# A mixture-of-experts decoder layer on one core: every weight row block split, one activation for the gate, slots found for four experts at a time

## The chip, the cores and the metric

The kernel runs on one core of one Trainium2 chip. The metric is the device time of one execution in microseconds, the median of several runs. The kernel before took 2383.85 us, the median of 3 runs (2383.01 to 2394.71).

## What is computed

One decoder layer over 1024 tokens of width 1024 in float32: a mixer (stick-breaking attention beside causal pooling), cross-attention into 256 memory tokens, and a mixture of experts, each behind an RMSNorm and a residual add; then a last RMSNorm. The change lies in the experts, where each token goes to 4 of 32 experts:

```
gu   = xb @ w1[e] + b1[e]                  # 1024 -> 2048, gate | up
gate = min(gu[:, :1024], 7);  up = clip(gu[:, 1024:], -7, 7)
act  = (up + 1) * gate * sigmoid(1.702 * gate)
y    = (act @ w2[e] + b2[e]) * g           # 1024 -> 1024, g = the routing weight
out[token] += y
```

## The kernel before

The first third of the run is the mixer, the cross-attention and the routing; the change does not touch it but for one scale factor. From about 830 us to the end the kernel goes through the 32 experts in the fixed order `ORDER`, by rank of load (rank 0 has the most tokens; `CAPS` gives each rank its capacity C, from 204 down to 128).

Each expert's weights (12 MB) come as 12 pieces of 1 MB: pieces 0 to 7 of `w1` (each 128 gate and 128 up columns), 8 to 11 of `w2` (256 columns each). A piece has 8 row blocks of 128 rows (index k, `KD` = 8). `load_split` (L1069) issues the load of a piece into a tile `wt` on SP's queue and then makes two parts of the first six row blocks (`KS` = 6): `wh` = the scaled weights in float32r, by ScalarE (L1073), and `wl` = the remainder in float16, by VectorE (L1074). The last two row blocks (`KW` = 2) are used whole, in float32, straight out of `wt`; so `wt` (6 buffers) stays taken until TensorE is through with the piece. `piece` (L1392) issues loads and splits `AHEAD` = 5 pieces ahead of the one that TensorE needs; `wh` and `wl` have 5 buffers each.

The 18 ranks with C over 128 run `ffn_wide` (L1184): weights are stationary, tokens stream. `packed` (L1115) makes one product of 128 output columns: six float32r matmuls over 2C columns (the tokens' high and low part side by side, L1123), six float16 matmuls over C (L1126), two float32 matmuls over C (L1129; each leaves two records in the trace). An expert has 16 such products for gate and up, 8 more for `w2`. Each gate/up product is brought out of PSUM by ScalarE and VectorE (L1198, L1200), clipped (L1203, L1204), gated (`gated`, L1077: a sigmoid on ScalarE, two multiplies on VectorE, L1080 and L1082), and its result parted again for the next product: a float32r copy on ScalarE (L1209), the remainder and a float16 copy on VectorE (L1210, L1055). The two row blocks j = 6, 7 that stay whole end with the gate (L1084). The `w2` products begin with `early` = 3 products over the first `ek` = 5 row blocks, so that the last gates have time to finish.

The other 14 ranks (C = 128) run `ffn_split` (L1256): tokens are stationary, weights stream. `mm_s` (L1132) does three matmuls of 256 columns for each split row block (L1137, L1138, L1139), one float32 matmul for each whole one (L1141, two records).

`prep` (L1352) runs for expert i + 2 at the end of the fourth part of expert i's first product: `slots` (L142) finds which token sits in which slot of the expert (a comparison on VectorE, L144, small matmuls into PSUM, L154, then some nine VectorE instructions of one to three columns for each 128 slots, L160 to L175), and GpSimd gathers the tokens' rows. The rows are transposed and parted for the next expert by `x_T` and `parted` (L1017, L1041; L1049 copies the whole blocks). The instructions' order on each engine is fixed by the tile framework, which simulates the program; `first(n)` raises the priority of what stands in it.

Of the kernel before, what the change touches and what calls it, by code (L numbers as in the profile page):

```python
# [22 lines left out]
P = 128  # L23
# [4 lines left out]
NE = 32  # L28
# [15 lines left out]
           'xg0'), tags=0, BB=(3,), avs=(0, 1), PS=(2, 3, 2), LAG=1, AB=2, GB=(2,), ORD3=range(0, 8), m3=28, mulL=0, x16=1, a16=0, a16L=1, early=3, ek=5, prep=3, wt=6, wh=5, wl=5,  # L44
# [4 lines left out]
KS = 6  # L49
KW = 8 - KS  # L50
# [9 lines left out]
def block_kernel(ctx: ExitStack, tc: tile.TileContext, x, mem, win, gcol, grow, wpool, wout, wqT, wkv, wo,  # L60
# [81 lines left out]
    def slots(C, iota, pcolr, valr, oh, pt, sl, idx, pin=False, later=None, unit=1.0):  # L142

        one = nc.vector.tensor_tensor(oh[:, :, :C], iota[:, None, :C].to_broadcast([P, NB, C]),  # L144
                                      pcolr[:, :, None].to_broadcast([P, NB, C]), op=OP.is_equal)
        if pin:
            tc.keep_in_program_order(one)
# [787 lines left out]
    for i in range(2):  # L935
        r = ORDER[i]
        with tc.issue_after(last.ins):
            S0[i] = slots(CAPS[r], iota_s, posM[:, :, r], lambda b, r=r: vals[:, b, r],
                          sm.tile([P, NB, 256], BF, name="t4", bufs=1) if i else rcs.tile([P, NB, P], BF, name="oh0"),
                          ps.tile([P, 2, 8], F32, name="pl", bufs=2),  # L940
                          rcs.tile([P, 2, 8], F32, name=f"sl{i}"), rcs.tile([P, 2, 2], I32, name=f"idx{i}"), later=later, unit=1.0 / WS)
# [75 lines left out]
    def x_T(sb, q, xg, C):  # L1017

        if general[0]:
            xT = sb.tile([P, KD, P], F32, name="xT")  # L1020
        else:
            xT = sb.tile([P, KS, 2 * C], F32R, name="xT")
            x16 = sb.tile([P, KS, C], F16, name="x16")
            xw = sb.tile([P, KW, C], F32, name="xw")

        def part(g, h):
# [8 lines left out]
            else:  # L1035
                with first(PLAN['hd']):
                    parted(pt[:, :, :m], 4 * h, xT[:, :, o:o + m], xT[:, :, C + o:C + o + m], x16[:, :, o:o + m],
                           xw[:, :, o:o + m], PLAN['x16'])
        return xT if general[0] else (xT, x16, xw), [lambda g=g, h=h: part(g, h) for g in range(len(xg)) for h in range(2)]

    def parted(src, k0, hi, lo, h16, whole, e):  # L1041

        n = max(0, min(4, KS - k0))
        if n:
            ks = slice(k0, k0 + n)
            split(hi[:, ks], lo[:, ks], src[:, :n])
            half(h16[:, ks], hi[:, ks], e)
        if n < 4:
            nc.scalar.activation(whole[:, k0 + n - KS:k0 + 4 - KS], src[:, n:], AF.Copy, scale=WS)  # L1049
# [19 lines left out]
    def load_split(w, src, eng=None):  # L1069
        t = load(w, src, eng)  # L1070
        hi = w.tile([P, KS, 256], F32R, name="wh", bufs=PLAN["wh"])
        lo = w.tile([P, KS, 256], F16, name="wl", bufs=PLAN["wl"])
        last_a[0] = nc.scalar.activation(hi, t[:, :KS], AF.Copy, scale=WS).ins  # L1073
        nc.vector.scalar_tensor_tensor(lo, t[:, :KS], WS, hi.bitcast(F32), op0=OP.mult, op1=OP.subtract)  # L1074
        return hi, lo, t

    def gated(sb, out, g, u, sg, eng=0, unit=None):  # L1077

        nc.scalar.activation(sg, g, AF.Sigmoid, scale=ALPHA)
        nc.vector.scalar_tensor_tensor(u, u, 1.0 - LIM, g, op0=OP.max, op1=OP.mult)  # L1080
        if unit is None:
            (nc.gpsimd if eng else nc.vector).tensor_tensor(out, u, sg, op=OP.mult)  # L1082
        else:
            nc.vector.scalar_tensor_tensor(out, u, unit, sg, op0=OP.mult, op1=OP.mult)  # L1084

    def ffn1(sb, q, w1u, xT, bcol):
        act = sb.tile([P, KD, P], F32, name="act", bufs=1)
        for j in range(8):
# [8 lines left out]
            gated(sb, act[:, j], t[:, 0], t[:, 1], sb.tile([P, 256], F32, name="sg")[:, :P])  # L1097
# [17 lines left out]
    def packed(q, C, part, cs, x, x16, xw, ps=None, ks=range(KD)):  # L1115

# [15 lines left out]
    def mm_s(ps, k, xhi, xlo, x16, xw, part, start, stop):  # L1132

        hi, lo, t = part
        kw = dict(skip_group_check=True)
        if k < KS:
            nc.tensor.matmul(ps, xhi[:, k], hi[:, k], start=start, stop=False, **kw)  # L1137
            nc.tensor.matmul(ps, xlo[:, k], hi[:, k], start=False, stop=False, **kw)  # L1138
            nc.tensor.matmul(ps, x16[:, k], lo[:, k], start=False, stop=stop, **kw)  # L1139
        else:  # L1140
            nc.tensor.matmul(ps, xw[:, k - KS], t[:, k], start=start, stop=stop, **kw)  # L1141
# [42 lines left out]
    def ffn_wide(sb, q, xT, need, r, C, sl, idx, between, last=False):  # L1184

        xT, x16, xw = xT
        act = sb.tile([P, KS, 2 * C], F32R, name="act", bufs=1)
        a16 = sb.tile([P, KS, C], F16, name="a16", bufs=1)
        aw = sb.tile([P, KW, C], F32, name="aw", bufs=1)
        for c in range(4):  # L1190
            for f in range(2):
# [3 lines left out]
                for g in range(2):  # L1195
                    ph = packed(q, C, part, slice(g * P, g * P + P), xT, x16, xw)
# [5 lines left out]
                with first(PLAN['hb']):  # L1202
# [40 lines left out]
        for eh in range(2):  # L1243
# [12 lines left out]
    def ffn_split(sb, q, xT, need, r, C, sl, idx, between, last=False):  # L1256
# [10 lines left out]
        def act_T(c):  # L1267
# [4 lines left out]
            if c % 2:  # L1272
                with first(PLAN['hf']):
                    parted(acts[-1][:, :, :C], 2 * c - 2, aT[:, 0], aT[:, 1], a16, aw,
                           PLAN['a16E'] if last else PLAN['a16L'])
        for c in range(4):
            ph = q.tile([P, 512], F32, name="qh", bufs=5)[:C]
            nc.tensor.matmul(ph, sel, b1hl[:, c], start=True, stop=False, skip_group_check=True)
            for h in range(2):
                part = need(2 * c + h)  # L1280
                for k in range(KD):
                    mm_s(ph[:, h * 256:h * 256 + 256], k, xT[:, :, :C], xT[:, :, C:], x16, xw, part, False,
                         h == 1 and k == KD - 1)
                settle()
            with first(PLAN['he']):
# [6 lines left out]
                gated(sb, ac, t[:, 0], t[:, 1], sb.tile([P, 256], F32, name="sg")[:C], PLAN["mulL"])  # L1292
# [11 lines left out]
        def products(eh, h, kh):  # L1304
# [4 lines left out]
            for k in range(4 * kh, 4 * kh + 4):  # L1309
                mm_s(py[eh][:, h * 256:h * 256 + 256], k, aT[:, 0], aT[:, 1], a16, aw, parts[eh, h], h == k == 0,  # L1310
# [227 lines left out]
```

## Time and profile before

| what | value |
|---|---|
| median of 3 runs | 2383.85 us |
| profiled execution | 2387.4 us, of which the span 2385.8 us |
| experts' stretch | about 830 us to the end |
| granted TensorE clock, mean | 0.972 |

PE is TensorE's matmuls, PEld its weight loads, DVE VectorE, ACT ScalarE, POOL GpSimd, SP the engine that issues most loads. Busy times of one engine in a stretch count overlapping instructions once; a row of grouped instructions gives the sum and the mean time of one, where neighbours can overlap.

### The profile page before, as it was taken

Reading aid. Unit: us, or ns where it says so; the run is one execution under the profiler, and the core shown is the slowest. Engines: PE = TensorE matmul, PEld = TensorE weight load, DVE = VectorE, ACT = ScalarE, POOL = GpSimd, SP = SyncE. Lnnn points to the kernel's source line nnn. Section 1 sums busy time; section 2 is a strip of 40 time slices with the busy share of each in tenths; the row PEclk is TensorE's granted clock in tenths of the full one; section 3 lists DMA queues with packets and bytes.
Section 4 is the critical chain, followed back from the end, with each engine's and each line's share of the span. In section 5 each row is a group of like instructions: output and inputs, shape, how many; then the busy total and the mean of one; then the engine's idle time right before and its main releaser. Section 6 shows DMA issues by size and latency. Waiting matters only on the chain. (4 is left out here: it accounts for less than half of the span.)

```text
span 2385.8 us, 44846 instructions
## 1 busy us (share of the span) xinstructions
PE 2233.9 (94%) x17218; PEld 2031.2 (85%) x17218; DVE 1685.1 (71%) x3716; ACT 1333.7 (56%) x2318; POOL 456.7 (19%) x387
## 2 busy tenths in 40 slices
PE   8999998899899889999999999999999999999985
PEld 7989886689899779988988889987988988888874
DVE  6752878764755667867887677776777777766775
ACT  6633565443542356656666566664666656655653
POOL 2101566543340000111010101101101101011001
PEclk9999999899999889999999999999999999999998
DMA  7821113154322368978778977987888788878785
GB/s 254 278 82 54 45 45 88 58 168 162 113 89 98 146 233 328 316 281 324 299 269 296 323 302 289 329 306 255 298 288 310 276 291 309 285 263 308 264 316 180
DMA packets 100461, 549.90 MB, mean 230 GB/s; under 512 B 14309, under 2 KB 18533, under 8 KB 48401
## 3 DMA queue, kind: packets, MB, share of 16 engines
q1 hardware_dynamic: 74016, 478.71, 53.6%
q0 software_dynamic: 15872, 46.21, 8.1%
q10 hardware_dynamic: 10354, 22.06, 2.6%
q8 instruction: 137, 2.24, 0.4%
q14 instruction: 82, 0.67, 0.1%
HBM read 493.16 MB, written 49.57 MB: 227 GB/s over the span
## 5 line engine op out<-in xcount | busy, mean ns | idle before, releaser
L1074 DVE SCALAR_TENSOR_TENSOR wl<-wt,wh 128x1536 f16<-128x1536 f32 x384 | 673.0, 1754 | 319.6 <-ACT wh L1073 308.8
L1073 ACT ACTIVATE wh<-wt 128x1536 fp32r<-128x1536 f32 x384 | 568.7, 1482 | 320.7 <-DMA wt<-w 291.9
L1123 PE MATMUL qh<-xT,wh 128*128 128x332 f32 (+17 forms) x1728 | 320.0, 321 | 5.6 <-ACT wh L1073 2.4
L1123 PEld LDWEIGHTS qh<-xT,wh 128*128 128x128 f32 x1728 | 255.0, 191 | 8.0 <-DVE gu L1200 3.3
L1137 PE MATMUL qh<-wh,xT 128*128 128x256 f32 x672 | 255.9, 382 | 0.6 <-ACT wh L1073 0.5
L1012 POOL DMA_INDIRECT xg<-Hdr,idx x50 | 58.4, 1168 | 805.2 <-DVE sl L175 322.2
L1129 PE MATMUL qh<-xw,wt 128*128 128x166 f32 (+17 forms) x1152 | 210.2, 304 | 0.0
L1126 PEld LDWEIGHTS <-wl 128*128 128x128 f16 x2592 | 173.1, 99 | 42.1 <-issue 4.6
L1101 POOL DMA_INDIRECT Adr<-y,idx x50 | 104.6, 2091 | 497.0 <-ACT y L1236 186.4
L1139 PE MATMUL qh<-wl,x 128*128 128x256 f16 x672 | 192.3, 286 | 6.7 <-DVE wl L1074 6.5
L1123 PE MATMUL qh<-act,wh 128*128 128x332 f32 (+17 forms) x864 | 179.0, 335 | 20.2 <-DVE act L1210 20.1
L1138 PE MATMUL qh<-wh,xT 128*128 128x256 f32 x672 | 191.5, 285 | 1.2 <-DVE xT L103 1.2
L1126 PE MATMUL qh<-x,wl 128*128 128x166 f16 (+17 forms) x1728 | 168.7, 231 | 0.0
L96 PE MATMUL pd<-uhi,Thi 128*128 128x256 f32 x576 | 165.7, 288 | 1.5 <-DVE x L617 1.1
L97 PE MATMUL pd<-ulo,Thi 128*128 128x256 f32 x576 | 163.7, 284 | 0.0
L1129 PEld LDWEIGHTS qh<-xw,wt 128*128 128x128 f32 x1152 | 162.5, 191 | 0.1
L98 PE MATMUL pd<-uhi,Tlo 128*128 128x256 f32 x576 | 162.5, 282 | 0.0
L1123 PEld LDWEIGHTS qh<-act,wh 128*128 128x128 f32 x864 | 134.6, 197 | 23.9 <-DVE act L1210 22.8
L1137 PEld LDWEIGHTS qh<-wh,xT 128*128 128x128 f32 x672 | 135.8, 202 | 13.9 <-issue 7.3
L1138 PEld LDWEIGHTS qh<-wh,xT 128*128 128x128 f32 x672 | 131.1, 195 | 3.9 <-DVE xT L103 1.5
L1137 PE MATMUL qh<-wh,act 128*128 128x256 f32 x336 | 124.0, 378 | 1.4 <-ACT act L102 1.4
L1198 ACT ACTIVATE gu<-qh,b1P 128x166 f32<-128x166 f32 (+17 forms) x288 | 104.7, 379 | 24.3 <-PE qh L1129 23.2
(398 smaller groups left out, 5506.2 us busy)
## 6 DMA issues: line engine op xcount, KB each, us to landing
wt<-w SPq DMA_DIRECT2D x382, 1024.0 KB
w<-wkv SPq DMA_DIRECT2D x8, 1024.0 KB
uw<-wout SPq DMA_DIRECT2D x16, 512.0 KB
uw<-Mdr SPq DMA_DIRECT2D x16, 512.0 KB
w<-win SPq DMA_DIRECT2D x5, 1024.0 KB
xt<-x SPq DMA_DIRECT2D x8, 512.0 KB
w<-wqT SPq DMA_DIRECT2D x4, 1024.0 KB
Mdr<-st ACTq DMA_DIRECT2D x8, 512.0 KB
```

The lines of the kernel that those rows point to most:

```text
L96: nc.tensor.matmul(ps, whi, mhi, start=start, stop=False, **kw)
L97: nc.tensor.matmul(ps, whi, mlo, start=False, stop=False, **kw)
L98: nc.tensor.matmul(ps, wlo, mhi, start=False, stop=stop, **kw)
L1073: last_a[0] = nc.scalar.activation(hi, t[:, :KS], AF.Copy, scale=WS).ins
L1074: nc.vector.scalar_tensor_tensor(lo, t[:, :KS], WS, hi.bitcast(F32), op0=OP.mult, op1=OP.subtract)
L1123: nc.tensor.matmul(ps[:, :2 * C], part[0][:, k, cs], x[:, k], start=k == 0, stop=False, **kw)
L1126: nc.tensor.matmul(ps[:, :C], part[1][:, k, cs], x16[:, k], start=False, stop=False, **kw)
L1129: nc.tensor.matmul(ps[:, :C], part[2][:, k, cs], xw[:, k - KS], start=False, stop=k == KD - 1, **kw)
L1137: nc.tensor.matmul(ps, xhi[:, k], hi[:, k], start=start, stop=False, **kw)
L1138: nc.tensor.matmul(ps, xlo[:, k], hi[:, k], start=False, stop=False, **kw)
L1139: nc.tensor.matmul(ps, x16[:, k], lo[:, k], start=False, stop=stop, **kw)
L1198: nc.scalar.activation(t[:, g], ph[:, C:2 * C], AF.Identity, scale=1.0 / WS, bias=b1P[:, 8 * g + j, r:r + 1])
```

## The change

All eight row blocks of a piece are split (`KS`, `KW`, the whole tiles `xw`, `aw` and the float32 matmuls go). Loads and splits are separated: splits run 5 pieces ahead as before, loads 8 ahead, and `wt` has 4 buffers in place of 6, given back after the split. The gate is one Silu on ScalarE and one VectorE instruction; its factor 1/1.702 is put into the routing weight (`GU`). The float16 copy of the wide experts' activations moves from VectorE to ScalarE (`a16=1`). Slots are found for four experts in one PSUM tile: one expert's comparison and small matmuls in each of four experts' third part (`mark`), and one set of nine VectorE instructions for all four (`settle_set`).

```diff
-           'xg0'), ... mulL=0, x16=1, a16=0, a16L=1, early=3, ek=5, prep=3, wt=6, wh=5, wl=5,
+           'xg0'), ... mulL=0, x16=1, a16=1, a16L=1, early=3, ek=5, prep=3, wt=4, wh=5, wl=5, ahead=8,
-KS = 6
-KW = 8 - KS
+GU = 1.0 / (WS * ALPHA)
+SLOT_SETS = [[2, 3]] + [list(range(i, i + 4)) for i in range(4, 32, 4)]
...
-    def load_split(w, src, eng=None):
-        t = load(w, src, eng)
-        hi = w.tile([P, KS, 256], F32R, name="wh", bufs=PLAN["wh"])
-        lo = w.tile([P, KS, 256], F16, name="wl", bufs=PLAN["wl"])
-        last_a[0] = nc.scalar.activation(hi, t[:, :KS], AF.Copy, scale=WS).ins
-        nc.vector.scalar_tensor_tensor(lo, t[:, :KS], WS, hi.bitcast(F32), op0=OP.mult, op1=OP.subtract)
-        return hi, lo, t
-    def gated(sb, out, g, u, sg, eng=0, unit=None):
-        nc.scalar.activation(sg, g, AF.Sigmoid, scale=ALPHA)
-        nc.vector.scalar_tensor_tensor(u, u, 1.0 - LIM, g, op0=OP.max, op1=OP.mult)
...
+    def split_w(w, t):
+        hi = w.tile([P, KD, 256], F32R, name="wh", bufs=PLAN["wh"])
+        lo = w.tile([P, KD, 256], F16, name="wl", bufs=PLAN["wl"])
+        last_a[0] = nc.scalar.activation(hi, t, AF.Copy, scale=WS).ins
+        nc.vector.scalar_tensor_tensor(lo, t, WS, hi.bitcast(F32), op0=OP.mult, op1=OP.subtract)
+        return hi, lo
+    def gated(out, g, u, sg):
+        nc.scalar.activation(sg, g, AF.Silu, scale=ALPHA)
+        nc.vector.scalar_tensor_tensor(out, u, 1.0 - LIM, sg, op0=OP.max, op1=OP.mult)
...
         for k in ks:
-            if k < KS:
-                nc.tensor.matmul(ps[:, :2 * C], part[0][:, k, cs], x[:, k], start=k == 0, stop=False, **kw)
+            nc.tensor.matmul(ps[:, :2 * C], part[0][:, k, cs], x[:, k], start=k == 0, stop=False, **kw)
         for k in ks:
-            if k < KS:
-                nc.tensor.matmul(ps[:, :C], part[1][:, k, cs], x16[:, k], start=False, stop=False, **kw)
-        for k in ks:
-            if k >= KS:
-                nc.tensor.matmul(ps[:, :C], part[2][:, k, cs], xw[:, k - KS], start=False, stop=k == KD - 1, **kw)
+            nc.tensor.matmul(ps[:, :C], part[1][:, k, cs], x16[:, k], start=False, stop=k == KD - 1, **kw)
...
-                    if j < KS:
-                        ac = sb.tile([P, 256], F32, name="ac", bufs=PLAN["ac"])[:, :C]
-                        gated(sb, ac, t[:, 0], t[:, 1], sg)
-                        nc.scalar.activation(act[:, j, :C], ac, AF.Copy)
-                        nc.vector.tensor_tensor(act[:, j, C:], ac, act[:, j, :C].bitcast(F32), op=OP.subtract)
-                        conv(PLAN['a16'], a16[:, j], ac)
-                    else:
-                        gated(sb, aw[:, j - KS], t[:, 0], t[:, 1], sg, unit=WS)
+                    ac = sb.tile([P, 256], F32, name="ac", bufs=PLAN["ac"])[:, :C]
+                    gated(ac, t[:, 0], t[:, 1], sg)
+                    nc.scalar.activation(act[:, j, :C], ac, AF.Copy)
+                    nc.vector.tensor_tensor(act[:, j, C:], ac, act[:, j, :C].bitcast(F32), op=OP.subtract)
+                    conv(PLAN['a16'], a16[:, j], ac)
...
+        def mark(n, m):
+            if m == 0:
+                found[n] = q.tile([P, 4, 2, 8], F32, name="qs")
+                nc.tensor.matmul(found[n].rearrange("p m g c -> p (m g c)"), none[:, :P], none[:, :64], start=True,
+                                 stop=False, skip_group_check=True)
...
+            tc.keep_in_program_order(nc.vector.tensor_tensor(
+                oh, iota_s[:, None, :C].to_broadcast([P, NB, C]), posM[:, :, r, None].to_broadcast([P, NB, C]),
+                op=OP.is_equal))
+            for g in range((C + P - 1) // P):
+                w = min(P, C - g * P)
+                for b in range(NB):
+                    nc.tensor.matmul(found[n][:w, m, g, :6], oh[:, b, g * P:g * P + w], vals[:, b, r], start=False,
+                                     stop=False, skip_group_check=True)
+        def settle_set(n):
+            pt = found.pop(n)
+            sl = sb.tile([P, 4, 2, 8], F32, name="sl", bufs=3)
+            idx = sb.tile([P, 4, 2, 2], I32, name="idx", bufs=3)
+            nc.vector.tensor_copy(sl[:, :, :, :3], pt[:, :, :, :3])
+            nc.vector.tensor_scalar(sl[:, :, :, 3:6], pt[:, :, :, 3:6], GU, None, op0=OP.mult)
...
         def piece(i, j):
-            emit(i * 12 + j + 1 + AHEAD)
+            upto = i * 12 + j + 1 + AHEAD
+            while todo_s and todo_s[0][0] * 12 + todo_s[0][1] < upto:
+                n = todo_s.pop(0)
+                emit(n[0] * 12 + n[1] + 1)
+                pieces[n] = split_w(w, loaded.pop(n))
+            emit(i * 12 + j + 1 + PLAN["ahead"])
             return pieces.pop((i, j))
```

## Rows read from the trace of the kernel before

**Rows 1.** The page: span, busy time of each engine, SP's DMA queue (packets, MB, share).
```profile
span 2385.8 us, 44846 instructions
PE 2233.9 (94%) x17218; PEld 2031.2 (85%) x17218; DVE 1685.1 (71%) x3716; ACT 1333.7 (56%) x2318; POOL 456.7 (19%) x387
q1 hardware_dynamic: 74016, 478.71, 53.6%
```
**Rows 2.** Busy time by stretch: length, PE, PEld, DVE, ACT, POOL, clock, DMA share, GB/s.
```profile
830.00:880.00 50.00, 39.07 (x252) 31.89 (x251) 30.52 (x47) 28.09 (x35) 5.14 (x6) 0.79 0.72 267
...
2330.00:2386.00 56.00, 29.89 (x199) 25.19 (x197) 31.10 (x84) 20.47 (x39) 11.52 (x8) 0.80 0.52 171
sum 1556.00, PE 1463.42 PEld 1324.44 DVE 1156.28 ACT 944.92 POOL 173.41; mean PE 292.68 PEld 264.89 DVE 231.26 ACT 188.98 POOL 34.68
...
1260.70:1308.60 47.90, 45.80 (x419) 43.36 (x418) 38.13 (x92) 31.42 (x59) 4.53 (x3) 1.00 0.80 283
1308.60:1387.80 79.20, 76.52 (x578) 65.74 (x576) 58.02 (x98) 46.72 (x61) 9.00 (x5) 1.00 0.86 317
```
**Rows 3.** Waits of PE from 880 to 2340 us: total, times, longest.
```profile
PE qh L1123 <- DVE act L1210: 20.1, 10, 4.5
```
**Rows 4.** Timeline of PE in one wide expert, C = 148: start us, us, instructions.
```profile
1291.87 0.92 PE L1123 MATMUL qh<-act,wh 128*128 128x296 f32 x5
...
1292.92 0.92 PE L1123 MATMUL qh<-act,wh 128*128 128x296 f32 x5
...
1296.28 0.40 PE L1123 MATMUL qh<-act,wh 128*128 128x296 f32 x1 [2.10 <-DVE act L1210]
...
1304.98 1.07 PE L1123 MATMUL qh<-act,wh 128*128 128x296 f32 x6
1305.90 0.57 PE L1126 MATMUL qh<-a,wl 128*128 128x148 f16 x6
1306.30 0.71 PE L1129 MATMUL qh<-aw,wt 128*128 128x148 f32 x4
1306.75 1.07 PE L1123 MATMUL qh<-act,wh 128*128 128x296 f32 x6
```
**Rows 5.** Timeline of PE in one split expert.
```profile
1505.71 1.03 PE L1141 MATMUL qh<-wt,xw 128*128 128x256 f32 x4
...
1506.85 0.36 PE L1137 MATMUL qh<-wh,xT 128*128 128x256 f32 x1
...
1507.21 0.36 PE L1137 MATMUL qh<-wh,xT 128*128 128x256 f32 x1
...
1508.73 1.03 PE L1141 MATMUL qh<-wt,xw 128*128 128x256 f32 x4
```
**Rows 6.** Groups of DVE and ACT, 830 us on: busy, mean ns | idle before, releaser.
```profile
L1074 DVE SCALAR_TENSOR_TENSOR wl<-wt,wh 128x1536 f16<-128x1536 f32 x384 | 673.0, 1754 | 319.6 <-ACT wh L1073 308.8 <-PE qh L1139 4.7 <-ACT gu L1198 2.8
L1073 ACT ACTIVATE wh<-wt 128x1536 fp32r<-128x1536 f32 x384 | 568.7, 1482 | 320.7 <-DMA wt<-w 291.9 <-PE qh L1138 8.2 <-PE qh L1123 6.5
...
L1080 DVE SCALAR_TENSOR_TENSOR gu<-gu 128x256 f32<-128x256 f32 (+18 forms) x200 | 68.5, 342 | 2.0
...
L1209 ACT ACTIVATE act<-ac 128x166 fp32r<-128x166 f32 (+17 forms) x108 | 35.0, 325 | 16.3 <-DVE ac L1082 14.9 <-PE qh L1138 0.9
...
L1055 DVE CAST a<-ac 128x166 f16<-128x166 f32 (+17 forms) x108 | 25.8, 240 | 0.3
...
L160 DVE COPY sl<-qs 128x3 f32<-128x3 f32 (+17 forms) x47 | 5.5, 147 | 1.6 <-PE qs L154 1.5
...
L1079 ACT ACT_TABLE_LOAD x1 | 1.3, 1283 | 0.0
```
**Rows 7.** Timeline of DVE in the wide expert of rows 4.
```profile
1286.60 0.30 DVE L1080 SCALAR_TENSOR_TENSOR gu<-gu 128x148 f32<-128x148 f32 x1
1286.83 0.23 DVE L1055 CAST a<-ac 128x148 f16<-128x148 f32 x1
1286.97 0.30 DVE L1210 TENSOR_TENSOR act<-ac,act 128x148 fp32r<-128x148 f32 x1
...
1288.00 1.75 DVE L1074 SCALAR_TENSOR_TENSOR wl<-wt,wh 128x1536 f16<-128x1536 f32 x1
1289.67 0.23 DVE L1204 TENSOR_SCALAR gu<-gu 128x148 f32<-128x148 f32 x1
```

More of the change, by code (lines that the diff above doesn't have):

```diff
@@ L43 @@
            a16E=1, fb=((0, 1, 2), (3, 4), (5, 6), (7,)), fn=('xg1', 'y1', 'xg0', 'y0', 'xg1', 'y1', 'xg1',
-           'xg0'), tags=0, BB=(3,), avs=(0, 1), PS=(2, 3, 2), LAG=1, AB=2, GB=(2,), ORD3=range(0, 8), m3=28, mulL=0, x16=1, a16=0, a16L=1, early=3, ek=5, prep=3, wt=6, wh=5, wl=5,
+           'xg0'), tags=0, BB=(3,), avs=(0, 1), PS=(2, 3, 2), LAG=1, AB=2, GB=(2,), ORD3=range(0, 8), m3=28, mulL=0, x16=1, a16=1, a16L=1, early=3, ek=5, prep=3, wt=4, wh=5, wl=5, ahead=8,
            gu=2, ac=4)
@@ L140, in bcast_row, with slots @@
         return t
[L142 to L147, printed above, removed]
+    def slots(C, iota, pcolr, valr, oh, pt, sl, idx, later=None, unit=1.0):
+        nc.vector.tensor_tensor(oh[:, :, :C], iota[:, None, :C].to_broadcast([P, NB, C]),
+                                pcolr[:, :, None].to_broadcast([P, NB, C]), op=OP.is_equal)
         ng = (C + P - 1) // P
@@ L1037, in part, with parted @@
                     parted(pt[:, :, :m], 4 * h, xT[:, :, o:o + m], xT[:, :, C + o:C + o + m], x16[:, :, o:o + m],
[L1038 to L1049, printed above, removed]
+                           PLAN['x16'])
+        return xT if general[0] else (xT, x16), [lambda g=g, h=h: part(g, h) for g in range(len(xg)) for h in range(2)]
+    def parted(src, k0, hi, lo, h16, e):
+        ks = slice(k0, k0 + 4)
+        split(hi[:, ks], lo[:, ks], src)
+        half(h16[:, ks], hi[:, ks], e)
     def conv(e, out, src):
@@ L1113, in ffn2, with packed @@
         scatter(ys, idx, 0, P)
-    def packed(q, C, part, cs, x, x16, xw, ps=None, ks=range(KD)):
+    def packed(q, C, part, cs, x, x16, ps=None, ks=range(KD)):
         if ps is None:
@@ L1246, in ffn_wide @@
             cs = lambda e: slice(e % 2 * P, e % 2 * P + P)
-            early = {e: packed(q, C, parts[e // 2], cs(e), act, a16, aw, None, range(PLAN['ek'])) for e in range(PLAN['early'] if eh == 0 else 0)}
+            early = {e: packed(q, C, parts[e // 2], cs(e), act, a16, None, range(PLAN['ek'])) for e in range(PLAN['early'] if eh == 0 else 0)}
             for e in range(4):
-                py = packed(q, C, parts[e // 2], cs(e), act, a16, aw, early.get(e), range(PLAN['ek'] if e in early else 0, KD))
+                py = packed(q, C, parts[e // 2], cs(e), act, a16, early.get(e), range(PLAN['ek'] if e in early else 0, KD))
                 with first(PLAN['hc']):
@@ L1352, in prep @@
         def prep(i):
-            r = ORDER[i]
             if i in S0:
                 S[i] = S0[i]
-            else:
-                S[i] = slots(CAPS[r], iota_s, posM[:, :, r], lambda b: vals[:, b, r], *slot_tiles(sb, q), pin=True,
-                             unit=1.0 / WS)
-            XG[i] = gather(sb, S[i][1], CAPS[r])
+            XG[i] = gather(sb, S[i][1], CAPS[ORDER[i]])
+        found, when = {}, {}
+        for n, s_ in enumerate(SLOT_SETS):
+            for m in range(len(s_)):
+                at = [(0, m), (1, m)][n] if n < 2 else (s_[0] - 6 + m, 2)
+                when.setdefault(at, []).append(lambda n=n, m=m: mark(n, m))
+            when.setdefault([(0, 2), (2, 1)][n] if n < 2 else (s_[0] - 3, 2), []).append(lambda n=n: settle_set(n))
@@ L1367, in block_kernel @@
         pieces = {}
-        todo = [(i, j) for i in range(NE) for j in range(12)]
+        loaded = {}
+        todo, todo_s = ([(i, j) for i in range(NE) for j in range(12)] for _ in range(2))
         def expert_id(i):
@@ L1409, in between @@
                     XT[i + 1], todo_x[:] = x_T(sb, q, XG[i + 1], CAPS[ORDER[i + 1]])
+                for f in when.get((i, c), []):
+                    f()
                 if c == PLAN['prep']:
@@ L1461, in block_kernel @@
                 nc.vector.tensor_sub(g_x, g_x, vx[:, :, 3 + c])
[L1462 removed]
+            sl, idx = slots(P, iota_s, pos_x, lambda b: vx[:, b], *slot_tiles(sb, q), unit=1.0 / ALPHA)
             xT, parts = x_T(sb, q, gather(sb, idx, P), P)
```

68 lines of the change are left out of this document (36 added, 32 removed).

## The prediction, written before the changed kernel was run

> **What bounds the kernel now.** I began with the page's busy line and its span, then took busy times by stretch. From 830 us to the end TensorE (PE) is busy 1463 of 1556 us, VectorE (DVE) 1156, ScalarE (ACT) 945 [rows 1, 2]. Of PE's 93 idle us, 11 lie in the first 50 us and 26 in the last 56; the 1450 us between hold 56. So the experts go at PE's pace, and DVE and ACT have room on the mean. The list of PE's waits says where the 56 us are: 20 us, the largest item, in 10 stops where the second product of a wide expert waits for the last parted activations, the longest 4.5 us [rows 3]. I call that place the handover. The groups by line show ACT idle 292 us before a split for the weights' landing and DVE idle 309 us behind ACT [rows 6]; neither reaches PE as a wait of that size, because splits run five pieces ahead. DMA is 80% busy in a wide expert and 86% in a pair of split ones [rows 2]. The fine timeline of PE then gives the price of each kind of matmul.
>
> **PE, wide experts.** A product with six split and two whole blocks takes 1306.75 - 1304.98 = 1.77 us, of which the four float32 records take 0.45 from their start to the next product [rows 4]. What eight split blocks cost stands in the trace too, since the early products run five split blocks and nothing else: 1292.92 - 1291.87 = 1.05 us, 0.21 a block [rows 4]. Three more blocks: the six float32r matmuls take 0.92 and the six float16 ones 0.40, 0.22 a block together, so 1.05 + 0.66 = 1.71 at most. The first float32r matmul of a run carries a start-up that further ones don't: 5 of them last 0.92 from the first start to the last end, 6 last 1.07, so one more is at most 0.15, and the streamed columns alone (296 and 148 at 2.4 GHz, the granted 1.00) are 0.185; with 0.20 the product is 1.65. Saved: 0.06 to 0.15 us; I take 0.11. There are 18 experts x 24 = 432 products, and the mean C (152.6) is near this 148: 432 x 0.11 = 48 us (26 to 65).
>
> **PE, split experts.** From float32 group to float32 group a piece takes 1508.73 - 1505.71 = 3.02 us, and one split block 1507.21 - 1506.85 = 0.36 [rows 5]. Eight blocks make 2.88; saved 0.14 us on 14 x 12 = 168 pieces, 23 us (18 to 28, as the handover from float32 back costs more or less). PE in all: -71 us, of 1463. Transposes and slot matmuls stay in number, but for one empty matmul a set (eight in all).
>
> **DVE.** A split grows from 1536 to 2048 elements. The row gives 1754 ns; in proportion that adds 585 ns; against the 0.30 us of a 148-element instruction of the same operation [rows 7] the slope is 1.05 ns an element, adding 536. I take 0.54: 384 x 0.54 = +207 us. The gate loses one of two instructions, 68 us; the float16 copies leave, 26 us [rows 6]. Two row blocks more per wide expert need a remainder: 36 x 0.30 = +11. Of x_T and of the split experts' activations the second half has four blocks for two: 64 x 256 elements x 1.05 ns = +17. Nine small slot instructions for each of 47 groups at 0.147 us, 62 us, become nine for each of eight sets, 14 at 0.2 us (they are wider): -48. Net +93: 1249.
>
> **ACT.** The split: 1482 ns, in proportion +494; against 325 ns at about 153 elements [rows 6] +428. I take 0.43: +165 us. Float16 copies for 144 row blocks and 36 new float32r copies at 0.325: +58. Silu for Sigmoid: same shape, 0. Two copies in place of one whole copy at x_T: +5. Net +228: 1173. If DVE and ACT were hidden behind PE as before, all this is free; the cover is PE's time. In a wide expert one row block j costs PE 2 x 1.66 = 3.32 us. DVE's, start to start [rows 7]: split 1.67 + 0.54, two PSUM reads, one gate instruction and one remainder at 0.23, two clips at 0.14 (the float16 copy's spacing): 3.41. Before it was 1.67 + 4 x 0.23 + 2 x 0.14 + 0.75 x (0.14 + 0.23) = 3.15 against PE's 3.54. So in the first product DVE goes from faster than PE to about even, and regains it in the second, where a piece needs no gate. That is thin cover.
>
> **What is late next: the handover.** PE's early products cover it as before: three of 1.05 us. Row blocks 6 and 7 now leave the gate by one DVE instruction less (-0.30) but then need a float32r copy on ACT (+0.33) and a remainder on DVE (+0.30): +0.33 us bare. Each new hop can stand behind a split, now about 1.9 us on ACT and 2.3 on DVE; with the engines 78% and 83% busy, half a split at that chance is 0.74 + 0.95. So +0.3 to +2.0 us in each of 18 wide experts, 6 to 36; I take 20. The same in split experts is wider by 256 elements on both engines: 14 x 0.3 = 4. For other queueing on fuller engines I take 4 more (0 to 30).
>
> **Loads.** Before, a load waited for PE to finish the piece six back. Now it waits for the split of the piece four back, and the split for PE's piece five back; loads reach eight pieces ahead. Queued on SP behind such a load are later loads, the reload of expert numbers and, near the end, result rows; on ACT, behind a split that waits for `wh`, the PSUM copies (L1198) that free PE's five buffers. I take 0: landing waits shift to waits for PE's buffers, and PE has four split pieces in hand. Bounds: -25 (more room between the wide and the split experts' demand removes half of the 56 us) to +30. The slots come earlier and gathers with them; no PE wait in the rows is theirs: 0. Other tiles' sizes: 0.
>
> **Sum.** 2387.4 - 48 - 23 + 20 + 4 + 4 = 2344 for an execution like the profiled one, which lies 3.5 us above the median of the runs; on the median's scale 2341. PE would then be 1392 of about 1513 us, DVE 83%, ACT 78%.
>
> **A rule against it.** The trace has a single table load in this part, 1.283 us, ahead of the first Sigmoid, and after it copies, scaled copies and Sigmoid mix without another [rows 6]. The Trainium skill ("ScalarE: Activation LUTs", "Table sets: the hidden batching unit") says functions come in sets, a change of set costs a load, and cheap ones such as copy and identity are in every set; it doesn't list Silu's. By its last part the change is free, which is the sum above; if Silu's set lacked the copies, it is the last rival.
>
> **Rivals.**
> 1. The new depth pays: handovers don't get longer (DVE rid of 48 us of slot work, PE never short of split pieces) and half the 56 us go. 2384 - 71 - 5 = 2308 to 2315. For it: the 292 us that ACT spends on landings. Against: DVE even with PE. Chance 0.18.
> 2. DMA takes over in the split experts. A 1 MB piece costs 0.536 x 2385.8 / 478.71 x 1.0486 = 2.80 us at full use [rows 1]; a split expert's share of 0.86 over 39.6 us is 34 us of transfers, with gathers and scatters. At 37.9 us that is 0.90. If no more than the present 0.86 can be had there, the split experts' 23 us are lost, and some 8 for unevenness: 2341 + 23 + 8 = 2372. Against: deeper loads even it out. Chance 0.11.
> 3. The handover eats the gain: each of 18 wide experts stops for the longest seen, 4.5 us, 81 us for 20: 2384 - 71 + 61 = 2374, no change. Chance 0.10.
> 4. Slower: DVE becomes the bound of the wide experts' first product. Its place is the eight row blocks at 3.41 us and the comparison and transposed halves (about 3 us) against PE's 26.6 and transposes; from the point where DVE's block exceeds PE's, PE runs out of its five buffers and then waits at the handover for all of DVE's backlog. At 4.5 + 2.0 us per wide expert it is 117 - 20 = 97 us, and half of the 384 splits 0.1 us late 19: 2384 - 71 + 97 + 19 = 2429 at worst, 2400 in the middle. It decides where DVE's spacing is over some 3.5 us a block. Chance 0.09.
> 5. Table changes: two loads of 1.283 us for each of 200 gates put 513 us on ACT, 1686 for 1556: about 2384 + 170 = 2550. Chance 0.02.
>
> **How the numbers follow.** The forecast (2325 to 2360) has 0.50. A measurement tells 0.5%, about 12 us, from no change, so faster means below 2372: the forecast, rival 1 and half of rival 2, 0.74 in all; same is rival 3 and the rest of 2, 0.15; slower is 4 and 5, 0.11. The range for 8 in 10 is 2305 (all of PE's saving and the recovered waits) to 2385.
>
> **What would show it.** PE's wide products 1.66 us apart and a split piece at 2.88; L1074 and L1073's successors at about 2.29 and 1.91 us, 384 each; no second table load; PE's waits for the last remainders 35 to 45 us in total; ACT's idle for landings far under 292. I am wrong if a product saves under 0.06 us, if DVE is over 90% busy in wide experts with PE waits over 100 us, or if DMA is over 0.9 busy with PE waiting for `wh` and `wl`.

## The result: no gain, 0.6% slower

The changed kernel takes 2403.33 us (median of 7 runs, 2396.41 to 2408.48), the kernel before 2387.39 beside it: a ratio of 1.0064 (95% interval 1.0045 to 1.0083). The forecast was 2341. The page after, as in [rows 1], and the stretch from 830 us, as the sum in [rows 2]:

```profile
span 2400.3 us, 45219 instructions
PE 2191.6 (91%) x17562; PEld 1988.5 (83%) x17562; DVE 1806.0 (75%) x3094; ACT 1527.2 (64%) x2434; POOL 502.4 (21%) x387
q1 hardware_dynamic: 74016, 478.71, 54.1%
```
```profile
880.00:1380.00 500.00, 458.19 (x4029) 413.90 (x4029) 411.52 (x626) 365.65 (x547) 66.64 (x67) 0.96 0.80 290
...
sum 1572.00, PE 1418.02 PEld 1279.58 DVE 1278.51 ACT 1139.70 POOL 218.58; mean PE 283.60 PEld 255.92 DVE 255.70 ACT 227.94 POOL 43.72
```

PE works 45 us less, DVE 122 more, ACT 195 more, and the span is 14.5 us longer. PE's unit prices are the predicted ones. Timelines of PE (start, duration): a wide product at C = 148 follows the one before after 1291.44 - 1289.77 = 1.67 us (forecast 1.66; before 1.77), and a split block comes 0.37 us after the one before (0.36 in the median), eight to a piece. Over all 18 wide experts, first products at full clock and without a stop follow each other 0.10 us sooner than before on the mean; such pieces of the split experts take 2.91 us for 3.04 in the median.

```profile
1289.77 1.33 PE L1111 MATMUL qh<-xT,wh 128*128 128x296 f32 x8
1290.94 0.70 PE L1113 MATMUL qh<-x,wl 128*128 128x148 f16 x8
1291.44 1.33 PE L1111 MATMUL qh<-xT,wh 128*128 128x296 f32 x8
```
```profile
1334.98 0.36 PE L1120 MATMUL qh<-wh,xT 128*128 128x256 f32 x1
...
1335.35 0.36 PE L1120 MATMUL qh<-wh,xT 128*128 128x256 f32 x1
```

The groups of DVE and ACT, as in [rows 6] (busy, mean ns | idle before, releaser):

```profile
L1068 DVE SCALAR_TENSOR_TENSOR wl<-wt,wh 128x2048 f16<-128x2048 f32 x384 | 875.2, 2285 | 169.7 <-ACT wh L1067 165.6 <-PE qh L1113 3.1
L1067 ACT ACTIVATE wh<-wt 128x2048 fp32r<-128x2048 f32 x384 | 732.7, 1913 | 172.8 <-PE qh L1121 68.4 <-DMA wt<-w 56.4 <-PE qh L1111 39.2
L1074 DVE SCALAR_TENSOR_TENSOR ac<-gu,sg 128x256 f32<-128x256 f32 (+18 forms) x200 | 67.1, 339 | 1.8 <-ACT sg L1073 0.5
L1073 ACT ACT_TABLE_LOAD x1 | 1.3, 1283 | 0.0
```

The splits cost what was expected, and ACT's idle for landings went from 292 to 56 us. There is still one table load in this part. The Trainium skill ("ScalarE: Activation LUTs", "Table sets: the hidden batching unit") says that cheap functions such as copy and identity are in every set; the single load agrees with that, and shows it beside Silu, which the section's list of sets doesn't name.

What changed is who makes PE wait (880 to 2340 us: total, times, longest):

```profile
PE qh L1111 <- DVE gu L1180: 32.7, 20, 3.1
PE qh L1111 <- DVE act L1189: 15.9, 18, 4.1
PE qs L1343 <- DVE oh L1337: 10.1, 10, 4.6
PE qt L1212 <- DVE yT L1229: 9.9, 14, 1.0
```

The longest single stop comes late, behind this window, and ends at 2355 us: PE waits there for ACT to write a wide expert's `y`. The kernel before has none like it:

```profile
PE qt L1247 <- ACT y L1213: 10.9, 1, 10.9
```

The handover, feared in the forecast (35 to 45 us), fell from 20.1 us [rows 3] to 15.9. The new first item is PE's five buffers, freed by DVE's read L1180; before, that item (L1200) was 2.2 us. One such stop, in DVE's and then PE's timeline:

```profile
1250.61 2.28 DVE L1068 SCALAR_TENSOR_TENSOR wl<-wt,wh 128x2048 f16<-128x2048 f32 x1
1252.81 0.28 DVE L1074 SCALAR_TENSOR_TENSOR ac<-gu,sg 128x130 f32<-128x130 f32 x1
1253.02 2.28 DVE L1068 SCALAR_TENSOR_TENSOR wl<-wt,wh 128x2048 f16<-128x2048 f32 x1
1255.22 0.28 DVE L1189 TENSOR_TENSOR act<-ac,act 128x130 fp32r<-128x130 f32 x1
1255.42 0.48 DVE L1180 SCALAR_TENSOR_TENSOR gu<-qh,gu 128x130 f32<-128x130 f32 x2
```
```profile
1255.85 1.95 PE L1111 MATMUL qh<-xT,wh 128*128 128x260 f32 x8 [2.24 <-DVE gu L1180]
...
1260.38 1.20 PE L1111 MATMUL qh<-xT,wh 128*128 128x260 f32 x8
```

Two splits stand back to back, the reads wait behind them, and PE stops for 2.24 us. Then the same eight matmuls take 1.95 us for 1.20. The windows of 1 us show why (length, PE, PEld, DVE, ACT, POOL, clock, DMA, GB/s): PE is busy 0.15 us in the first, and the granted clock stands at 0.50 (1.2 GHz) for the next three.

```profile
1255.00:1256.00 1.00, 0.15 (x1) 0.18 (x2) 1.00 (x6) 0.19 (x2) 0.00 (x0) 0.99 0.99 414
1256.00:1257.00 1.00, 1.00 (x6) 1.00 (x7) 1.00 (x7) 0.00 (x0) 0.90 (x1) 0.50 1.08 451
...
1260.00:1261.00 1.00, 1.00 (x14) 1.00 (x14) 1.00 (x1) 0.87 (x4) 0.00 (x0) 1.00 0.66 213
```

The whole of this wide expert's first product before and after (windows from its first to its last float32r matmul, columns as above):

```profile
1215.40:1242.30 26.90, 26.90 (x272) 25.91 (x271) 22.93 (x60) 20.92 (x43) 4.60 (x2) 1.00 1.00 342
```
```profile
1231.20:1261.60 30.40, 28.16 (x277) 26.80 (x276) 27.28 (x49) 26.38 (x51) 5.79 (x3) 0.94 0.95 347
```

DVE's work in it rose from 22.9 to 27.3 us, more than the 26.9 that the stretch lasted before, when PE never stopped in it.

**The balance.** From 830 us to PE's last matmul, PE's idle time grew from 71.2 to 123.8 us (+53). The time at 1.2 GHz grew from 62.3 to 118.8 us, and what PE was busy of it from 54.4 to 98.3 us. If half of that is lost, as at half the clock, matmuls took 22 us longer (an estimate). Less that, PE's work fell by 45 + 22 = 67 us (forecast 71; from the unit prices above, 432 x 0.10 + 168 x 0.13 = 65). From PE's last matmul to the end it is 28.5 us for 21.1, +7. In sum -67 + 53 + 22 + 7 = +15, the change of the span.

### The profile page after: what moved, and what is told of

Same layout as the page of the kernel before. It is cut to its first block, busy times and chain, and to the rows that moved or that the text cites. A ratio compares the mean times of both kernels' runs of the same rounds, so it can differ in the third digit from the quotient of the medians.

```text
span 2400.3 us, 45219 instructions
## 1 busy us (share of the span) xinstructions
PE 2191.6 (91%) x17562; PEld 1988.5 (83%) x17562; DVE 1806.0 (75%) x3094; ACT 1527.2 (64%) x2434; POOL 502.4 (21%) x387
## 3 DMA queue, kind: packets, MB, share of 16 engines
q8 instruction: 140, 2.29, 0.4%
## 5 line engine op out<-in xcount | busy, mean ns | idle before, releaser
L1068 DVE SCALAR_TENSOR_TENSOR wl<-wt,wh 128x2048 f16<-128x2048 f32 x384 | 875.2, 2285 | 169.7 <-ACT wh L1067 165.6
L1067 ACT ACTIVATE wh<-wt 128x2048 fp32r<-128x2048 f32 x384 | 732.7, 1913 | 172.8 <-PE qh L1121 68.4
L1111 PE MATMUL qh<-xT,wh 128*128 128x332 f32 (+17 forms) x2304 | 407.0, 318 | 32.0 <-DVE gu L1180 31.8
L1111 PEld LDWEIGHTS qh<-xT,wh 128*128 128x128 f32 x2304 | 336.4, 193 | 37.3 <-issue 32.2
L1120 PE MATMUL qh<-wh,xT 128*128 128x256 f32 x896 | 334.9, 375 | 6.7 <-ACT wh L1067 6.7
L1122 PE MATMUL qh<-wl,x 128*128 128x256 f16 x896 | 258.0, 288 | 6.2 <-DVE wl L1068 6.2
L1121 PE MATMUL qh<-wh,xT 128*128 128x256 f32 x896 | 256.7, 287 | 3.4 <-DVE xT L104 3.4
L1111 PE MATMUL qh<-act,wh 128*128 128x332 f32 (+17 forms) x1152 | 229.3, 333 | 16.9 <-DVE act L1189 15.9
L1111 PEld LDWEIGHTS qh<-act,wh 128*128 128x128 f32 x1152 | 180.4, 201 | 23.0 <-DVE act L1189 20.1
L1120 PEld LDWEIGHTS qh<-wh,xT 128*128 128x128 f32 x896 | 183.5, 205 | 16.2 <-ACT wh L1067 7.8
L1121 PEld LDWEIGHTS qh<-wh,xT 128*128 128x128 f32 x896 | 176.7, 197 | 4.6 <-DVE xT L104 3.6
L1120 PE MATMUL qh<-wh,act 128*128 128x256 f32 x448 | 159.6, 368 | 0.8 <-ACT act L103 0.8
L1122 PE MATMUL qh<-wl,a 128*128 128x256 f16 x448 | 128.0, 288 | 1.9 <-DVE wl L1068 1.9
L1121 PE MATMUL qh<-wh,act 128*128 128x256 f32 x448 | 128.9, 294 | 0.8 <-DVE act L104 0.8
L1122 PEld LDWEIGHTS <-x 128*128 128x128 f16 x896 | 87.2, 97 | 39.0
```

The lines of the kernel that those rows point to most:

```text
L1067: last_a[0] = nc.scalar.activation(hi, t, AF.Copy, scale=WS).ins
L1068: nc.vector.scalar_tensor_tensor(lo, t, WS, hi.bitcast(F32), op0=OP.mult, op1=OP.subtract)
```

## The experiments

Ratios are to the kernel before on the same chip, in brackets the 95% interval. The theory at first: DVE's and ACT's fuller queues hold up PE. The rivals: the loads, the slots or the gate.

**The parts alone, with six split blocks.**

```diff
-        nc.scalar.activation(sg, g, AF.Sigmoid, scale=ALPHA)
-        nc.vector.scalar_tensor_tensor(u, u, 1.0 - LIM, g, op0=OP.max, op1=OP.mult)
...
+        nc.scalar.activation(sg, g, AF.Silu, scale=ALPHA)
+        nc.vector.scalar_tensor_tensor(out, u, (unit or 1.0) * (1.0 - LIM), sg, op0=OP.max, op1=OP.mult)
```


> The kernel before with the Silu gate alone (six of eight row blocks split, slots as before). Theory A, long splits queue in front of the PSUM reads: VectorE has 68 us less to do and no split grows, so PE's waits shrink a little, 2372 to 2387 us. Rival B, the gate or the slot sets cost the time by their order on the engines: 2395 or more here or in the next run. PE's waits for the PSUM reads (none over 3 us in total in the kernel before) stay under 5 us by A.

Measured 2371.05 us, 0.9921 [0.9897, 0.9944], just under theory A's range.

```diff
-                S[i] = slots(CAPS[r], iota_s, posM[:, :, r], lambda b: vals[:, b, r], *slot_tiles(sb, q), pin=True,
-                             unit=1.0 / WS)
...
+        def mark(n, m):
+        def settle_set(n):
...
+                for f in when.get((i, c), []):
+                    f()
```


> The kernel before with the slot sets alone. Theory A: some 40 us less on VectorE, no split grows, 2374 to 2388 us. Rival B: the comparisons and small matmuls of a set stand at places where PE waits for them (10 us of waits of L1343 for L1337 in the changed kernel, each followed by a stretch at the half clock), 2395 or more.

Measured 2377.55 us, 0.9949 [0.9933, 0.9965], as by theory A.

Both edits together:

> The kernel before with the Silu gate and the slot sets, six of eight row blocks split. Theory A: over 100 us less on VectorE and all splits as short as before: 2362 to 2383 us, the fastest so far. Rival B: 2395 or more. Rival C, PE's own time with the whole float32 blocks is the bound and no relief of VectorE helps: 2380 to 2390.

Measured 2355.98 us, 0.9856 [0.9823, 0.9889], under all ranges. Each part pays, and they add up. What is left of the change, eight split blocks with the loads in two steps and the float16 copy on ACT, turns 0.9856 into 1.0064: it costs about 50 us. With six blocks neither the gate nor the slots cost time. With eight, PE's waits for the slots' comparisons come to 10.1 us, for 0.2 us here; no run takes the sets alone out of the changed kernel.

**The splits in halves, with eight blocks.** Both lines, or one of the two:

```diff
-        last_a[0] = nc.scalar.activation(hi, t, AF.Copy, scale=WS).ins
-        nc.vector.scalar_tensor_tensor(lo, t, WS, hi.bitcast(F32), op0=OP.mult, op1=OP.subtract)
+        for ks in (slice(0, 4), slice(4, 8)):
+            last_a[0] = nc.scalar.activation(hi[:, ks], t[:, ks], AF.Copy, scale=WS).ins
+            nc.vector.scalar_tensor_tensor(lo[:, ks], t[:, ks], WS, hi[:, ks].bitcast(F32), op0=OP.mult, op1=OP.subtract)
```


> The changed kernel with each split in two instructions on each engine (row blocks 0 to 3, then 4 to 7), so that a PSUM read never stands behind more than some 1.2 us of split, for about 0.15 us more VectorE and ScalarE time a piece (58 us each in all). Theory A, the length of what stands in front: PE's waits for the PSUM reads fall from 33 us to under 12 and the time to 2365 to 2390. Rival D, VectorE's and ScalarE's total work: more work makes it slower, 2405 to 2430.

Measured 2346.6 us, 0.9835 [0.9798, 0.9873], below both ranges. The sign that theory A gave is not there: PE's wait for the reads falls from 32.7 us to 21.8 and not under 12, and the handover rises from 15.9 to 25.0.

```profile
PE qh L1112 <- DVE act L1190: 25.0, 17, 4.3
PE qh L1112 <- DVE gu L1181: 21.8, 15, 2.3
```

> The changed kernel with VectorE's split alone in two instructions, ScalarE's whole. Theory A (what matters is how long a PSUM read or the last remainder stands behind a split on VectorE): most of the gain of half_splits, 2350 to 2372 us. Theory E (what matters is that VectorE can begin on the first half while ScalarE makes the second, which this kernel doesn't allow): 2390 to 2410, and VectorE's idle time behind ScalarE's split stays near 166 us.

Only DVE's: 2395.13 us, 1.0023 [1.0001, 1.0044], in theory E's range.

> The changed kernel with ScalarE's split alone in two instructions, VectorE's whole. Theory A as above (VectorE is the queue): little gain, 2390 to 2405 us. Theory A2 (the PSUM reads stand behind ScalarE's split, which is first in their chain): 2350 to 2375. Theory E: 2390 to 2410, since VectorE still waits for both halves.

Only ACT's: 2388.33 us, 1.0002 [0.9986, 1.0018], 2 us under the ranges of A and E.

The group of DVE's split, in the order both, DVE's, ACT's:

```profile
L1069 DVE SCALAR_TENSOR_TENSOR wl<-wt,wh 128x1024 f16<-128x1024 f32 x768 | 910.5, 1219 | 84.1 <-ACT wh L1068 78.4 <-PE qh L1114 1.7 <-PE qh L1123 1.6
```
```profile
L1069 DVE SCALAR_TENSOR_TENSOR wl<-wt,wh 128x1024 f16<-128x1024 f32 x768 | 903.4, 1219 | 129.2 <-ACT wh L1067 126.6 <-PE qh L1114 1.5
```
```profile
L1069 DVE SCALAR_TENSOR_TENSOR wl<-wt,wh 128x2048 f16<-128x2048 f32 x384 | 876.0, 2287 | 153.2 <-ACT wh L1068 148.1 <-PE qh L1114 4.0
```

DVE's wait behind ACT's split is 166 us after the change, 127 (expected near 166) and 148 with one side halved, 78 with both. Both halves add work (DVE +27 us, ACT +29) and still save 57. Only with both can DVE begin a piece's first half while ACT makes its second: in series a piece then needs about 1.05 + 2 x 1.22 = 3.5 us instead of 1.91 + 2.29 = 4.2 (an estimate from these rows), while one side alone lengthens it (1.91 + 2 x 1.22, 2 x 1.05 + 2.29).

**More pieces.** The loop above with four slices of two blocks:

> The changed kernel with each split in four instructions of two row blocks on both engines. Theory A: the waits for PSUM reads and for the last remainders shrink once more, 2322 to 2345 us. Theory D: each further instruction adds work on VectorE (half_splits had 27 us more than the changed kernel, this some 80): 2360 to 2390. Theory E: near half_splits, 2340 to 2360.

Measured 2352.63 us, 0.9838 [0.9798, 0.9877], as with halves and as by theory E. The wait falls to 40 us, and DVE's work rises by 49 (sums from 830 us, halves first):

```profile
sum 1620.00, PE 1391.00 PEld 1259.59 DVE 1305.89 ACT 1168.44 POOL 215.15; mean PE 1391.00 PEld 1259.59 DVE 1305.89 ACT 1168.44 POOL 215.15
```
```profile
sum 1620.00, PE 1395.01 PEld 1264.26 DVE 1355.28 ACT 1230.79 POOL 224.62; mean PE 1395.01 PEld 1264.26 DVE 1355.28 ACT 1230.79 POOL 224.62
```

**More or moved work, with eight blocks.** The old gate put back:

```diff
-        nc.scalar.activation(sg, g, AF.Silu, scale=ALPHA)
-        nc.vector.scalar_tensor_tensor(out, u, 1.0 - LIM, sg, op0=OP.max, op1=OP.mult)
+        nc.scalar.activation(sg, g, AF.Sigmoid, scale=ALPHA)
+        nc.vector.scalar_tensor_tensor(u, u, 1.0 - LIM, g, op0=OP.max, op1=OP.mult)
+        nc.vector.tensor_tensor(out, u, sg, op=OP.mult)
...
```


> The changed kernel with the old gate (Sigmoid, two VectorE multiplies), 68 us more VectorE work, splits whole. Theory D (with all blocks split, VectorE's work sets the pace): 2445 to 2475 us, far more than the 18 us that the same work was worth with six blocks. Theory A (the length of one split in the queue) or E (splits come late): 2410 to 2432.

Measured 2448.52 us, 1.0237 [1.0194, 1.0281], as by theory D. The same instructions that are worth 0.8% with six blocks are worth 1.7% with eight, some 41 us. DVE is busy 61 us more; its wait behind ACT takes up 22 of them (166 to 144), and PE pays in the buffer wait:

```profile
PE qh L1112 <- DVE gu L1181: 54.3, 22, 5.2
PE qh L1112 <- DVE act L1190: 12.5, 15, 3.2
```

The float16 copy back on DVE, which moves work from ACT:

```diff
-... a16=1, a16L=1, early=3, ...
+... a16=0, a16L=1, early=3, ...
```


> The changed kernel with the float16 copy of the wide experts' activations back on VectorE (144 copies, some 33 us more there, 46 us less on ScalarE). Theory D: 2418 to 2435 us. If ScalarE's queue is as much the cause: 2385 to 2400. Theory A alone: 2398 to 2410.

Measured 2400.47 us, 1.0049 [1.0026, 1.0071]: no difference to the changed kernel, and so not theory D's 2418 or more. DVE works 24 us more and waits 30 less behind ACT's splits (166 to 136). For this copy it made no difference on which of the two engines it stands; together with the gate's run that speaks for one chain of both.

**Order and loads, with eight blocks.**

```diff
-... wt=4, wh=5, wl=5, ahead=8,
+... wt=4, wh=5, wl=5, ahead=5,
```


> The changed kernel with loads 5 pieces ahead as the splits, in place of 8 (four buffers as in the changed kernel). Theory T (near the end, results' rows wait on SP's queue behind loads that wait for a split, which held ScalarE's writing of y and with it PE for 10.9 us): that wait goes and the time falls by 8 to 18 us, 2385 to 2396; the rest of the stretch stays. Rival: the deeper loads keep PE fed, then 2410 or more, with ScalarE's waits for landings rising from 56 us to over 200.

Measured 2399.36 us, 1.0043 [1.0024, 1.0062], in neither range; the late stop behind ACT's `y` is 8.4 us for 10.9. As a cause of the loss, the longer lead of the loads is out.

```diff
-        nc.vector.scalar_tensor_tensor(lo, t, WS, hi.bitcast(F32), op0=OP.mult, op1=OP.subtract)
-        return hi, lo
+        later = lambda: nc.vector.scalar_tensor_tensor(lo, t, WS, hi.bitcast(F32), op0=OP.mult, op1=OP.subtract)
+        return (hi, lo), later
...
```


> The changed kernel with VectorE's split of a piece put into the program one piece after ScalarE's, so that it should find ScalarE's half of the work done; splits whole as in the changed kernel. Theory E (VectorE stands in its queue behind ScalarE's split, and PSUM reads stand behind VectorE): its wait for ScalarE falls from 166 us to under 90 and the time to 2345 to 2375 us. Theory A (the length of a split alone) or D (total work): 2395 to 2410.

Measured 2401.21 us, 1.0051 [1.003, 1.0071]. Inconclusive: DVE's wait behind ACT's split stayed at 161 us, so the later place in the program did not make the condition that it was to test.

```diff
-AHEAD = 5
+AHEAD = 6
-... wt=4, wh=5, wl=5, ahead=8,
+... wt=2, wh=6, wl=6, ahead=8,
```


> The changed kernel with the splits 6 pieces ahead in place of 5 (six buffers for the two parts, two for the loads). Theory E: PE's stops shrink and the time falls to 2350 to 2388 us. Theories A and D: 2393 to 2412, or more if two load buffers are too few (then ScalarE's waits for landings rise from 56 to over 150 us).

Measured 2786.39 us, 1.1661 [1.1614, 1.1707]. Two load buffers starve ACT, as its split's group shows, so this says nothing on one piece more of lead:

```profile
L1067 ACT ACTIVATE wh<-wt 128x2048 fp32r<-128x2048 f32 x384 | 733.7, 1911 | 533.5 <-DMA wt<-w 524.7 <-SPq L1460 4.8 <-DVE gu L1183 2.5
```

**The combination, and its neighbours.** Six blocks with Silu and the sets, the splits in two slices of three blocks:

```diff
+        for ks in (slice(0, 3), slice(3, 6)):
+            last_a[0] = nc.scalar.activation(hi[:, ks], t[:, ks], AF.Copy, scale=WS).ins
+            nc.vector.scalar_tensor_tensor(lo[:, ks], t[:, ks], WS, hi[:, ks].bitcast(F32), op0=OP.mult, op1=OP.subtract)
```


> Silu gate and slot sets with six of eight row blocks split (silu_sets_6of8), each split in two instructions of three row blocks on both engines. If the length of a split in front of a PSUM read costs time only where VectorE is nearly full, nothing is gained on silu_sets_6of8: 2352 to 2368 us. If it costs everywhere: 2338 to 2350. In the first case all eight blocks split is worth some 10 us beside it, in the second nothing.

Measured 2332.24 us, 0.975 [0.9711, 0.9789]: the fastest of all, and under both ranges, so a split in one piece costs time with six blocks too. PE does 1439 us of work, 48 more than with eight blocks in halves, and is idle 35 us instead of 83 to its last matmul.

Three slices of two blocks:

> Silu gate, slot sets, six of eight row blocks split in three instructions of two. If VectorE's waits behind ScalarE fall further (261 us in half_splits_6of8) by more than its work grows (some 30 us): 2318 to 2332 us. If PE is the bound there (35 us of stops left in the stretch): 2328 to 2342.

Measured 2335.68 us, 0.9766 [0.9735, 0.9798], the same.

Seven blocks, the splits in four and three:

```diff
-... wt=6, wh=5, wl=5,
+... wt=5, wh=5, wl=5,
-KS = 6
+KS = 7
...
```


> Silu gate, slot sets, seven of eight row blocks split in two instructions (4 and 3 row blocks), one float32 block; five load buffers for six, for room. PE's matmuls are some 36 us less than with six. If VectorE's work plus its waits behind ScalarE's split set the time (as in all runs with eight), it lies between half_splits_6of8 and half_splits, 2333 to 2348 us. If PE is still the bound at seven: 2300 to 2325.

Measured 2407.71 us, 1.0082 [1.0056, 1.0107], outside both expectations. PE's largest wait is the handover, 39.3 us in 26 stops. It also has one load buffer less, and the two are not separated; ACT's 234 us of waits for landings don't tell, since half_splits_6of8 has 248:

```profile
PE qh L1122 <- DVE act L1212: 39.3, 26, 4.2
```
```profile
L1076 ACT ACTIVATE wh<-wt 128x1024 fp32r<-128x1024 f32 (+1 forms) x768 | 687.0, 943 | 236.9 <-DMA wt<-w 234.1 <-SPq L1480 1.4
```

**The tail.** The halves again, in a single run, and then with another buffer for a late result block:

```diff
-... 'xg1', 'y1', 'xg1',
+... 'xg1', 'xg0', 'xg1',
```


> half_splits once more, one look, as the mark for the next two: 2335 to 2358 us, with PE's stop of some 11 us for ScalarE's y at 2278 us and some 38 us from PE's last matmul to the end.

One time, 2352.97 us.

> half_splits with the sixth final row block in a buffer of xg0 in place of y1, so that the last wide expert's y does not wait until that block's result row has left. Theory T2 (that row stands on SP's queue behind an earlier row, whose norm VectorE does late): PE's stop of 11 us and the later scatter go, 2318 to 2335 us. Rival: the stop is taken by another buffer, 2340 to 2352.

Measured 2348.82 us, 0.983 [0.9789, 0.987], as by the rival.

> half_splits_6of8 with the same exchange of one buffer. By T2 it gains little, since there the row leaves in time (PE's stop there is 4.8 us): 2322 to 2333 us. If all eight blocks split are worth anything at all, half_splits_y is under this one; by PE's own saving alone (71 us of matmuls for some 50 us more of stops) the two lie within 10 us of each other.

Measured 2337.1 us, 0.9799 [0.9759, 0.9838], above its range, and half_splits_y is not under it. With eight blocks PE's stop of 11.4 us before L1248 is gone, but from PE's last matmul to the end it is 45 us for 38. Nothing is gained; what sets the tail stays open.

## Why the prediction was wrong

PE's terms were right (-67 for -71), and so were the splits' prices, the gate's tables, the landings. The sum failed at what was to hide the work on DVE and ACT. Worked out from the traces: the time of the 18 wide experts' first products (first to last float32r matmul, with all that PE does between; in brackets busy PE and DVE), of their second products, and the rest from 830 us to PE's last matmul.

```
kernel             first products         second   rest
before             620.6 (615.2, 484.6)   322.3    591.8
silu_sets_6of8     592.5 (591.6, 447.8)   319.7    590.8
after              645.6 (604.8, 562.8)   321.6    574.6
gate_sigmoid       682.1 (619.7, 586.4)   326.6    581.6
half_splits        618.6 (596.0, 566.5)   314.6    541.2
quarter_splits     646.8 (607.2, 606.2)   296.2    542.7
half_splits_6of8   595.0 (592.1, 461.8)   299.7    579.6
half_splits_7of8   577.7 (566.6, 472.8)   364.2    605.0
```

1. **The failed step** is "If DVE and ACT were hidden behind PE as before, all this is free; the cover is PE's time", with its terms "For other queueing on fuller engines I take 4 more (0 to 30)" and half a split at the handover. Of the 53 us that PE's idle time grew, 36 lie in the first products (5.3 to 40.8 us), 3 in the second and 14 in the rest, 11 of these in the late stop. From silu_sets_6of8 to the changed kernel, which has the same gate and slots, the first products, which should save 288 x 0.10 = 29 us, lose 53, and the rest saves 16 (the forecast for split experts was 23 less 4). These two lengths don't compare as they stand: PE's work between the first products, most of it for a neighbouring expert, is 61 us in silu_sets_6of8 and 81 in the changed kernel. Less these 20 us, the first products lose 33 and the rest saves nothing. Without stops the first products would last about 592 - 29 + 20 = 583 us, and DVE has 563 us of work in them: 20 us are left for standing behind ACT's split, and DVE stood idle 83. With six blocks it is 448 of 592, and PE is busy 99.9%. With quarters DVE's work alone is 606 us, and the first products last as long as with whole splits. The halves take 27 us off the first products, 7 off the second and 33 off the rest: splits in one piece cost time outside the first products too. There, PE's waits for the two parts of a split expert's weights fall with the halves from 13.4 to 6.2 us, and those for DVE's `yT` (L1229) from 9.9 to 0.4.

2. **DVE's idle time was read as room.** The 309 us of [rows 6] stand in DVE's own order: while it waits for ACT's split, the reads that free PE's buffers stand behind it. From a product's last matmul to the end of DVE's read the mean over 288 products is 4.05 us before, 5.65 after, 4.98 with halves, 3.58 in half_splits_6of8. It is 5.62 in gate_sigmoid, which is 45 us slower than the changed kernel, so this delay alone doesn't give the time. The forecast's spacing of 3.41 us a row block counted instructions alone, without this wait and without the transposed halves and comparisons, which it named only in rival 4. Its shares of 83% and 78% are means over stages.

3. **Rival 4**, priced at 2400 in the middle, is what happened, in the place that it named: DVE in the first products. It named PE's five buffers too: in 11 of the 18 first products PE stops for 2 us or more, and the longest stop ends in the last 7 us of the stretch, ten times behind a read and once, for 4.6 us, behind a slot comparison. But its price lay on a backlog at the handover, which fell; that its 2400 is near 2403 is luck.

4. **The stops' second price** had no term: an estimated 22 us at half the clock. The end of the run was taken at 0 ("near the end, result rows") and cost 18 us: the late stop of 10.9 and the 7 behind PE's last matmul. The handover's 20 us came to -4.

5. **DVE's own sum** was +93 and came to +122. The gate gave 52 us (silu_6of8) and not 68, the slots 18 (sets_6of8) and not 48. The durations of small instructions overlap: in [rows 7] one of 0.30 us is followed after 0.23. ACT came to +195 for +228.

6. **The warning sign**, DVE "over 90% busy in wide experts with PE waits over 100 us", was met: PE's stops from 880 to 2340 us come to 101 us, and in 8 of the 18 first products DVE is over 90% busy (mean 87%). But expert by expert the busy share doesn't tell where PE stops. Six of the eight, at 92 to 93%, last 27 to 28 us, no longer than before, and PE is idle 0.4 us at most in each; of the ten others, nine have 2.2 to 5.2 us of idle PE. The six hold little of PE's other work (0.6 to 1.3 us each); eight of the nine that hold 7 us or more stop.

That DVE's and ACT's order is the cause is shown by the halves (more work on both, less standing, 57 us less) and by the gate (the same work costs twice as much with eight blocks). No run raised the reads over a split in DVE's order or gave PE more than five buffers; what either would give stays open. Whether one more piece of lead, or seven blocks with enough load buffers, would collect PE's saving was not settled.

## What to carry to other kernels

Compare a helper engine's work with the bound engine's time inside the stage that shares them, not over the span, and count as taken the time in which it stands in order behind another engine: only what is left is cover. If two engines work on one tile after the other, cut the work into two instructions on both, so that the second can start early; cutting one side alone did little. Run the parts of a change apart: two of three paid here, and the largest saving on the bound engine was the one to leave out: with the splits halved, six blocks take 2332 us and eight 2347.

## What the runs showed of the hardware

- An ACT split of 2048 elements a partition takes 1913 ns, one of 1024 takes 1052: cutting it in two costs 0.19 us. On DVE it is 2285 and 1219, 0.15 us.
- A stop of PE of 2.24 us was followed by some 3 us at 1.2 GHz with PE fully busy. Over the experts PE was busy 44 us more at that clock than before; if half of it is lost, that is 22 us (an estimate) beside 53 us of added idle time.
